# Layer B's queries, keys and P^T turned by VectorE and moved through DRAM, its q/k block number 3 projected sooner, and group 0's scores of layer A in full fp32

## The chip, the cores and the metric

The kernel runs on one core of a Trainium2 chip. The core has a matrix engine (TensorE, PE in the profile, with its weight loads shown as PEld), a vector engine (VectorE, DVE), a scalar engine (ScalarE, ACT), a general engine (GpSimd, POOL) and a queue, SyncE (SP), that issues nearly all DMA transfers here. The engines run side by side, each through its own instructions in order, and wait for each other by semaphores. The metric is the time of one execution on the device in microseconds; the time before is 845.8 us, the median of 3 runs (845.26 to 847.01).

## The reference

A block of two layers on 512 tokens of 1024 features, 16 heads of 64 in fp32. Each layer normalises x, projects it, mixes tokens by attention, multiplies with silu(gate), projects back and adds to x.

```python
def mixer_a(hn, w_in, w_out, q_gain, k_gain, t5_bias):
    proj = hn @ w_in                       # 3 groups of q, k, v and one gate
    for g, (window, dilation) in enumerate(((128, 1), (512, 4), (2048, 16))):
        q = rms_norm(qkv[:, :, g, 0], q_gain[g])
        k = rms_norm(qkv[:, :, g, 1], k_gain[g])
        o, lse = dilated_group_attention(q, k, v, t5_bias[...], dilation, reach)
    y = sum over g of softmax(lse over g) * o
    return (y * silu(gate)) @ w_out

def mixer_b(hn, w_in, w_out, q_gain, k_gain, rpb):
    q, k, v, gate = split(hn @ w_in, 4)    # q and k are normalised per head
    # tokens lie on an 8 x 64 grid; a query sees all 8 rows and a window of 16 columns
    logits = q . k + bias(row offset, column offset)
    p = softmax(logits)
    return ((p @ v) * silu(gate)) @ w_out
```

## The kernel before

The 16 heads are worked in 8 pairs (`hc` 0 to 7), a pair being 128 columns. Layer A is done pair by pair (`main_a`); layer B projects blocks in the order of `B_PARTS` (lines 38 to 41): "qk" i is q and k of pairs 2i and 2i+1 (512 columns), "v" i is v of four pairs, "gate" i is one pair's gate. Each projection contracts 8 steps of 128 rows.

Weights come from DRAM as blocks of 128 x 1024 floats (`wraw`, three buffers, line 184). Each half of a block is split in two parts that TensorE multiplies in its reduced fp32 form (`float32r`): a high part `wh` by ScalarE (line 132) and the rest `wl` by VectorE or GpSimd (line 138), four buffers each. A product is then three matmuls, high x high, high x low and low x high (`mm3`; `mm3_heads` for the two heads of a pair, each on 64 rows of the array). A few products are in full fp32 with unsplit operands.

TensorE's order is written out by hand. Two generators run against each other: `main` issues the projections and output products, `side` issues the attention. A clock kept by the program (`matmul`, `transpose`) adds a planned time per TensorE instruction, and `side` goes on when that clock has reached a due time: `yield "wait", key, delay` waits for a stamp plus a delay in planned nanoseconds. `later_on(delay, job)` puts work of other engines (a transfer, a scaling) at such a time. The order of the other engines is made by a scheduler, apart from instructions pinned with `keep_in_program_order`. A transfer on SP waits in its place in the queue until what it needs is there, and everything behind it waits too.

Layer A, per pair: the projected q is normalised, turned in 32 x 32 blocks by VectorE (`turn_q`), written to DRAM and read back (`move_q`), which leaves it transposed; pairs 6 and 7 are turned by TensorE instead (`transpose4`, line 219). Group 0's q and k are then split (`split_q`, `put_k`) into `q0h`, `q0l`, `k0h`, `k0l`, and scored with `mm3_heads`; groups 1 and 2 are scored in full fp32 with 32 queries a matmul, eight matmuls side by side on 64 x 32 parts of the array. `scores(u)` handles half of the tokens, so that there are 16 such units in the layer. P is turned by VectorE, sent to DRAM and read back into `pt` (`turner`, lines 770 to 783); pair 7's is turned by TensorE. `weigh` multiplies P^T with v (tile `o`).

Layer B, per pair (`side_b`): queries and keys (`raw`) are transposed by TensorE, four transposes each, into PSUM; ScalarE and VectorE read them from there, reordering the grid (`mid_rc`, `edge_rc`) and splitting into high and low parts; two units of scores follow, then softmax. P^T goes through DRAM for pairs 0 to 5 (`far`); for 6 and 7 TensorE transposes P (`turn_p`) and VectorE copies it to `pt` (line 1131). The bias of a pair is read by `bias_b` in six transfers from two small tables (lines 748 and 753). The output product (`out_product`) accumulates k-steps 0 to 6 of seven tiles before step 7, the last pair's, and then the eighth tile in halves.

P's trip in `side_b` reads, with the delays in planned nanoseconds:

```python
                turned.put(pr, 512 if u == 0 else 384, 224 * hd + 128 * u)
            later_on(9000, partial(turned.send, pt[:, :1792], 9500, 1200))
            pending.append(lambda: put_y(hc, weigh(), False, False))
```

Of the kernel before, what the change touches and what calls it, by code (L numbers as in the profile page):

```python
# [27 lines left out]
KT = 8  # L28
# [11 lines left out]
    ("qk", 2), ("v", 1), ("qk", 3), ("gate", 4), ("gate", 5), ("gate", 6), ("gate", 7),  # L40
# [6 lines left out]
def tile_hybrid_encoder(  # L47
# [26 lines left out]

    mid_rc = lambda t: sb(t, 64, [[128, 3], [1, 8], [8, 16]])
    edge_rc = lambda t: sb(t, 0, [[448, 2], [1, 8], [8, 8]])
    mid_q = lambda t: sb(t, 0, [[128, 3], [16, 8], [1, 16]])
    edge_q = lambda t: sb(t, 384, [[64, 2], [8, 8], [1, 8]])
    mid_o = lambda t: sb(t, 64, [[128, 3], [16, 8], [1, 16]])
    edge_o = lambda t: sb(t, 0, [[448, 2], [8, 8], [1, 8]])  # L80
    mid_cr = lambda t: sb(t, 64, [[128, 3], [1, 16], [16, 8]])
    edge_cr = lambda t: sb(t, 0, [[448, 2], [1, 8], [8, 8]])
    mid_n = lambda t: sb(t, 64, [[128, 3], [8, 16], [1, 8]])
    edge_n = lambda t: sb(t, 0, [[448, 2], [8, 8], [1, 8]])

# [12 lines left out]
    lb_d = dr.tile([P, 376], F32, name="lb_d")  # L98
    gb_d = dr.tile([P, 248], F32, name="gb_d")
# [41 lines left out]
    def blocks():  # L141
# [10 lines left out]
        yield from outs(A_OUT)  # L152
# [5 lines left out]
        yield from outs(B_OUT)  # L158

    def outs(b):  # L160

        for n, ks in ((512, KT - 1), (384, KT - 1), (512, 1), (384, 1), (128, KT)):
            yield b, n, ks
            b += n * ks
# [86 lines left out]
    def project(stat_h, stat_l, n, evac, guard, need=None):  # L251

        acc = {i: ps_acc.tile([P, 512], F32, tag="acc", name="acc") for i in range(4)}
        for k in range(KT):
# [5 lines left out]
            h, l = next(wsteps)  # L260
            if need and k == 0:
# [21 lines left out]

    def squares(v, ss, i, ns):
        sq = wk.tile([P, 512], F32, tag="sq", name="sq")[:, : ns * 64]
        if len(v.shape) == 3:
            v = v.rearrange("p (a f) r -> p a f r", f=4)
            nc.gpsimd.tensor_mul(sq.rearrange("p (f a r) -> p a f r", f=4, a=4), v, v)
# [6 lines left out]
    later = []  # L295

    def head_norm(raw, ss, ns, held, delay=0, quick=False):

# [4 lines left out]
        def scale():  # L303
            for i in range(4):
                by = rs[:, i * ns : (i + 1) * ns].unsqueeze(2)
                if len(raw.shape) == 4:
                    v = raw[:, :, i, :].rearrange("p (h a f) r -> p f h a r", h=2, f=4)
                    by = rs[:, i * ns : (i + 1) * ns].rearrange("p (f h) -> p f h", h=2)
                    by = by.unsqueeze(3).unsqueeze(4).to_broadcast([P, 4, 2, 2, 32])
# [4 lines left out]
                if held or delay:  # L314
                    tc.keep_in_program_order(m)

        if held:
            later.append(scale)
        elif delay:
            later_on(delay, scale)  # L320
        else:
            scale()
# [108 lines left out]
    def bias_rows():  # L431

        rp = wk.tile([P, 248], F32, tag="sq", name="rp")
        tc.keep_in_program_order(nc.sync.dma_start(rp, rpb))
        nc.gpsimd.tensor_scalar(rp, rp, -1.0, None, op0=ALU.mult)
        lb = wk.tile([P, 376], F32, tag="sq", name="lb")
        nc.gpsimd.memset(lb, BIG)
        nc.gpsimd.tensor_copy(lb[:, 15 * 8 : 31 * 8], rp[:, 7 * 8 : 23 * 8])
        nc.sync.dma_start(gb_d, rp)
        nc.sync.dma_start(lb_d, lb)  # L440

    st = {}
    pq = wk.tile([P, 4096], F32, tag="pt", name="pt", bufs=1)
    rk = wk.tile([P, 4608], F32, tag="rawk", name="rawk", bufs=1)
# [6 lines left out]
    def project_qk(n, ns, key, hc, guard, first=False, **kw):  # L451

        box = []

        def evac(i, acc):
            if not box:
                if key == "rawq":
# [3 lines left out]
                        if moved(hc)  # L461
# [5 lines left out]
                elif key == "v":  # L467
                    box.append(rk[:, 4 * n * hc : 4 * n * hc + 4 * n].rearrange("p (i c) -> p i c", i=4))
                else:
                    t = wk.tile([P, 4 * n], F32, tag="rawq", name=key, bufs=1)  # L470
                    box.append(t.rearrange("p (i c) -> p i c", i=4))
                box.append(None if key == "v" else wk.tile([P, 32], F32, tag="ss", name="ss"))
            raw, ss = box
            if key == "rawq" and moved(hc):
# [11 lines left out]
            if not first and key != "v":  # L486
                squares(raw[:, :, i, :] if key == "rawq" and moved(hc) else raw[:, i, : ns * 64], ss, i, ns)
# [10 lines left out]
        if key == "raw":  # L498

            ss2 = wk.tile([P, 32], F32, tag="ss", name="ss")  # L500
            for i in range(4):
                squares(raw[:, i, 256:], ss2, i, 4)
            head_norm(raw[:, :, :256], ss, 4, hc % 2 == 1, quick=True)
            head_norm(raw[:, :, 256:], ss2, 4, False, (16500, 16500, 14000, 16000)[hc])
            for n in range(2):
                st[key, 2 * hc + n] = raw[:, :, 256 * n : 256 * n + 256]
# [4 lines left out]
    def normed(raw, ss, ns, key, hc):  # L511
        head_norm(raw, ss, ns, False, 9000 if key == "rawk" and 0 < hc < NHC - 1 else 0)
# [63 lines left out]
    def q_tiles():  # L576
# [3 lines left out]
            wk.tile([P, 512], F32R, tag="q0h", name="q0h", bufs=1),  # L580
            wk.tile([P, 512], F32R, tag="q0l", name="q0l", bufs=1),
            wk.tile([P, 4, 4, P], F32, tag="q12", name="qt", bufs=1),
            wk.tile([P, EXT], F32R, tag="k0h", name="k0h", bufs=1),
            wk.tile([P, EXT], F32R, tag="k0l", name="k0l", bufs=1),
        )

    def q_a(hc):
# [6 lines left out]
        st["q", hc] = q0h, q0l, qt, k0h, k0l = q_tiles()  # L594

        tp = transpose4(raw, 0)
        nc.scalar.copy(tjr(q0h), to_tjr(tp))
        nc.vector.tensor_sub(tjr(q0l), to_tjr(tp), tjr(q0h.bitcast(F32)))
        yield
        tp = transpose4(raw, 3 * P)  # L600
        put_k([(trj(k0h[:, 64:EXT]), trj(k0l[:, 64:EXT]), to_trj(tp))], 0)
# [7 lines left out]
    def move_q(hc, raw):  # L609
# [3 lines left out]
        qt, left = tiles[2], [4]  # L613
# [25 lines left out]
    def split_q(q0h, q0l, qt, k0h, k0l):  # L639
        src = qt[:, :, 3, :].rearrange("p t (j r) -> p t r j", j=4)  # L640
        trj4 = lambda t: t[:, 64:EXT].rearrange("p (t r j) -> p t r j", t=4, j=4)
# [705 lines left out]
```

## Time and profile before

| | |
|---|---|
| time, median of 3 runs | 845.8 us (845.26 to 847.01) |
| span of the profiled execution | 843.7 us |
| what lies around the span, against the median | 2.1 us |
| TensorE busy | 837.7 us, 99% |
| VectorE / ScalarE / GpSimd busy | 528.4 / 427.8 / 294.2 us |
| DMA traffic | 141.20 MB, 167 GB/s mean |
| layer B, first projection to the end | about 569 to 844 us |

The span is the time from the first to the last instruction of one profiled execution; the page gives no other time of that execution. Rows of instruction groups name the line, the engine, the operation, out<-in by the program's names, shapes and a count, then busy time and mean duration, then the idle time of the engine before them and what ended it. In a timeline a row begins with start and duration in microseconds. The chain is the work followed back from the last instruction: at each step to what released it. The waits say which engine's line waited for which other line: total, times, longest.

### The profile page before, as it was taken

What the parts mean: (1) busy time and instruction counts of PE and PEld (TensorE: products, weight loads), DVE (VectorE), ACT (ScalarE), POOL (GpSimd) and SP (SyncE); (2) the same over time, 40 slices, a digit from 0 to 9 for tenths busy, and PEclk for the clock granted to TensorE, in tenths of its full rate; (3) what the DMA queues carried; (4) which work ended last, traced back from release to release, by engine and by line L of the source; (5) the groups of instructions that cost most, each with busy time, mean ns of one, the idle gap of its engine ahead of it and who ended that gap; (6) DMA issues with size and microseconds to landing.
All of it is one profiled execution on the core that took longest, in us unless ns stands there. A gap on an engine that the chain in (4) does not pass through costs nothing.

```text
span 843.7 us, 14965 instructions
## 1 busy us (share of the span) xinstructions
PE 837.7 (99%) x5378; PEld 676.3 (80%) x5378; DVE 528.4 (63%) x1371; ACT 427.8 (51%) x899; POOL 294.2 (35%) x432
## 2 busy tenths in 40 slices
PE   9999999999999999999999999999999999999998
PEld 7788888788788788788788787888878877777777
DVE  7354684684674674675674675447565777668653
ACT  7432653563553653652653564344366465664541
POOL 3352442452441541542532341121521625235211
PEclk9999999999999999999999999999999999999999
DMA  6345478378378278378276364164236546447323
GB/s 253 112 132 178 150 215 248 139 212 259 124 213 258 98 227 246 95 235 244 92 220 189 115 195 110 60 233 176 78 102 197 155 145 191 121 150 202 102 92 131
DMA packets 64218, 141.20 MB, mean 167 GB/s; under 512 B 5648, under 2 KB 23248, under 8 KB 64144
## 3 DMA queue, kind: packets, MB, share of 16 engines
q1 hardware_dynamic: 64000, 139.99, 54.0%
q8 instruction: 42, 0.69, 0.3%
q10 hardware_dynamic: 144, 0.26, 0.1%
q14 instruction: 32, 0.26, 0.1%
HBM read 109.11 MB, written 31.12 MB: 166 GB/s over the span
## 4 chain that ended last, share of the span: by engine, by line
PE 95%; DMA 2%; ACT 1%; DVE 1%; issue 0%; SPq 0%; ACTq 0%
PE acc L215 80%; PE log L215 5%; PE o L215 5%; PE tp L219 3%; DMA pt<-td 1%; DMA wraw<-in_w 1%; DVE hn_l L403 1%; ACT p L1119 1%; DMA x_all<-in_xt 0%; ACT p L694 0%; DVE pt L1017 0%; PE pa L215 0%; ACT raw L485 0%; PE pl L215 0%; PE pk L215 0%
## 5 line engine op out<-in xcount | busy, mean ns | idle before, releaser
L132 ACT CAST wh<-wraw 128x512 fp32r<-128x512 f32 (+1 forms) x259 | 158.3, 612 | 283.5 <-PE acc L215 246.0
L215 PE MATMUL acc<-wh,hn_h 128*128 128x512 f32 x704 | 282.4, 402 | 1.1 <-ACT hn_h L402 0.7
L215 PE MATMUL acc<-wh,hn_l 128*128 128x512 f32 x704 | 274.2, 390 | 0.0
L215 PE MATMUL acc<-wl,hn_h 128*128 128x512 f32 x704 | 274.1, 390 | 0.0
L138 POOL TENSOR_TENSOR wl<-wraw,wh 128x512 fp32r<-128x512 f32 (+1 forms) x104 | 135.2, 1300 | 366.1 <-ACT wh L132 344.5
L138 DVE TENSOR_TENSOR wl<-wraw,wh 128x512 fp32r<-128x512 f32 (+1 forms) x156 | 111.8, 717 | 146.4 <-ACT wh L132 145.3
L215 PEld LDWEIGHTS acc<-wh,hn_h 128*128 128x128 f32 x704 | 132.1, 188 | 35.8 <-issue 5.6
L215 PEld LDWEIGHTS acc<-wh,hn_l 128*128 128x128 f32 x704 | 132.2, 188 | 28.6
L215 PEld LDWEIGHTS acc<-wl,hn_h 128*128 128x128 f32 x704 | 132.4, 188 | 25.2 <-POOL wl L138 0.3
L215 PE MATMUL acc<-y,wh 128*128 128x512 f32 (+1 forms) x272 | 82.5, 387 | 0.0
L215 PE MATMUL acc<-hn_h,wh 128*128 128x512 f32 x192 | 76.1, 396 | 0.0
L215 PE MATMUL acc<-hn_h,wl 128*128 128x512 f32 x192 | 74.9, 390 | 0.0
L215 PE MATMUL acc<-hn_l,wh 128*128 128x512 f32 x192 | 74.8, 389 | 0.0
L694 ACT ACTIVATE p<-p,mn 128x512 f32<-128x512 f32 (+3 forms) x128 | 69.4, 585 | 0.6 <-DVE mn L693 0.2
L857 ACT ACTIVATE p<-p,mn 128x512 f32<-128x512 f32 (+1 forms) x64 | 44.8, 701 | 46.8 <-DVE mn L846 46.5
L291 DVE TENSOR_REDUCE ss<-sq 128x4 f32<-128x256 f32 (+1 forms) x96 | 48.3, 505 | 30.1 <-POOL sq L290 18.7
L770 DVE STREAM_TRANSPOSE tr<-p 128x512 f32<-128x512 f32 (+1 forms) x80 | 53.7, 683 | 12.3 <-ACT p L694 11.6
L215 PEld LDWEIGHTS acc<-y,wh 128*128 128x128 f32 x272 | 48.1, 189 | 9.6 <-issue 1.3
L215 PE MATMUL acc<-y,wl 128*128 128x512 f32 (+1 forms) x136 | 51.4, 378 | 0.0
L215 PEld LDWEIGHTS acc<-hn_h,wh 128*128 128x128 f32 x192 | 36.1, 188 | 8.0 <-issue 0.3
L215 PEld LDWEIGHTS acc<-hn_h,wl 128*128 128x128 f32 x192 | 36.0, 188 | 7.7
L215 PEld LDWEIGHTS acc<-hn_l,wh 128*128 128x128 f32 x192 | 36.1, 188 | 7.0
(143 smaller groups left out, 1041.1 us busy)
## 6 DMA issues: line engine op xcount, KB each, us to landing
wraw<-in_w SPq DMA_DIRECT2D x119, 512.0 KB
td<-tr SPq DMA_DIRECT2D x14, 1024.0 KB
pt<-td SPq DMA_DIRECT2D x56, 256.0 KB
qd<-rawq SPq DMA_DIRECT2D x6, 1024.0 KB
qt<-qd SPq DMA_DIRECT2D x24, 256.0 KB
td<-tr SPq DMA_DIRECT2D x6, 896.0 KB
pt<-td SPq DMA_DIRECT2D x24, 224.0 KB
e<-l_d SPq DMA_DIRECT2D x32, 112.0 KB
```

What stands on the lines that cost most here:

```text
L132: nc.scalar.copy(h, raw)
L138: eng.tensor_sub(l, raw, h.bitcast(F32))
L215: nc.tensor.matmul(o, l, r, **kw)
L219: nc.tensor.transpose(o, i, ident)
L291: nc.vector.tensor_reduce(ss[:, i * ns : (i + 1) * ns], sq.rearrange("p (a b) -> p a b", b=64), axis=AX.X, op=ALU.add)
L403: return nc.vector.scalar_tensor_tensor(l, xk, g, h.bitcast(F32), op0=ALU.mult, op1=ALU.subtract)
L694: nc.scalar.activation(pr, pr, AF.Copy, scale=mn[:, 3:4])
L770: nc.vector.transpose(dst, src[:, :n].rearrange("p (i b k) -> p i b k", b=4, k=32))
L857: nc.scalar.activation(row, row, AF.Exp, bias=mn[:, 1:2], scale=-1.0, accum_out=mn[:, 2:3])
L1119: nc.scalar.activation(pr[:, o : o + n], pr[:, o : o + n], AF.Exp, bias=mn[:, 0:1], scale=-1.0, accum_out=mn[:, 2:3])
```

## The change

1. *Layer B's queries and keys.* The projected block is laid out in 32-column blocks like layer A's q. For each pair VectorE turns it in 32 x 32 blocks in place (two stream transposes of 128 x 512), SP writes it to DRAM (`bd`) and reads it back in four transfers into a tile `landing`, where q and k lie transposed (`move_b`). The second pair of a block follows at a delay. ScalarE and VectorE split from `landing`; the eight q/k transposes of a pair on TensorE are gone. k's low part is made in four pieces, and a copy of q's first 64 tokens is appended, so that tokens stay in one order and the output is multiplied with the gate in one instruction.
2. *Layer B's P^T.* Pairs 6 and 7 go through DRAM as well; their products with v come between the steps of the output product, which now keeps the last two steps back (`late` 2).
3. *Order.* In `B_PARTS`, whose numbers count from 0, "qk" 3 stands behind a gate (24 matmuls) instead of behind "v" 1 (96 matmuls), and "v" 1 follows it. The delays of `side_b` are new.
4. *Projections and output product.* In the first two k-steps the fourth accumulator's matmuls come after the other three's.
5. *Bias of layer B.* During layer A 32 small transfers write a full table to DRAM (`eb_d`); each pair's bias is then read in one transfer instead of six.
6. *Layer A, group 0.* q and k are no longer split; the scores are full-fp32 products in the form of groups 1 and 2, with 256 or 192 columns of keys.

```diff
 B_PARTS = (
     ("qk", 0), ("v", 0), ("gate", 0), ("gate", 1), ("qk", 1), ("gate", 2), ("gate", 3),
-    ("qk", 2), ("v", 1), ("qk", 3), ("gate", 4), ("gate", 5), ("gate", 6), ("gate", 7),
+    ("qk", 2), ("gate", 4), ("qk", 3), ("v", 1), ("gate", 5), ("gate", 6), ("gate", 7),
 )
...
             h, l = next(wsteps)
+            if k < 2 and not need:
+                held.append((h, l))
+                for i in range(3):
+                    mm3(acc[i][:, :n], stat_h(k, i), stat_l(k, i), h, l, k == 0, False)
+                    yield
+                for j, (h, l) in enumerate(held if k else ()):
+                    mm3(acc[3][:, :n], stat_h(j, 3), stat_l(j, 3), h, l, j == 0, False)
+                    yield
+                continue
...
+        for c in range(16):
+            o = 120 - 8 * c
+            g = (56 if c < 8 else 120) - 8 * (c % 8)
+            later_on(15000 + 12000 * c, partial(write, 8 * c, 0, lb[:, o : o + 256]))
+            later_on(21000 + 12000 * c, partial(write, 8 * c, 256, rp[:, g : g + P]))
+    MOVE = 6000, 5500
...
-            head_norm(raw[:, :, :256], ss, 4, hc % 2 == 1, quick=True)
-            head_norm(raw[:, :, 256:], ss2, 4, False, (16500, 16500, 14000, 16000)[hc])
+            move = [partial(move_b, raw, 2 * hc + f) for f in range(2)]
+            head_norm(raw, ss, 4, 0, True, pair=0, then=move[0])
+            head_norm(raw, ss2, 4, (16500, 15000, 10000, 14000)[hc], pair=1, then=move[1])
...
+    def move_b(raw, hc):
+        n = hc % 2
+        blocks = raw.rearrange("p (a f) i r -> p a (f i r)", f=4)[:, :, 256 * n : 256 * n + 256]
+        for a in (0, 2):
+            nc.vector.transpose(blocks[:, a : a + 2], blocks[:, a : a + 2])
+        d = dr.tile([4, P, 256], F32, name="bd", tag="bd", bufs=2)
+        if "landing" not in st:
+            st["landing"] = wk.tile([P, 2, 4, 2, P], F32, tag="q12", name="landing", bufs=1)
+        place, left = st["landing"][:, n], [4]
+        def write():
+            tc.keep_in_program_order(nc.sync.dma_start(d.rearrange("a p x -> p a x"), blocks))
+            stamp["qk", hc] = 0
+        def read(a):
+            dst = place[32 * a : 32 * a + 32].rearrange("k t f x -> k t (f x)")
+            src = d[a].rearrange("(t k) x -> k t x", t=4)
+            tc.keep_in_program_order(nc.sync.dma_start(dst, src))
+            left[0] -= 1
+        later_on(MOVE[0], write)
+        for a in (0, 2, 1, 3):
+            later_on(MOVE[0] + MOVE[1], partial(read, a))
...
-                mm3_heads(
-                    [lg[:, cs : cs + n] for lg in lgs],
-                    lambda hs: q0h[hs, qs], lambda hs: q0l[hs, qs],
-                    lambda hs: k0h[hs, ks], lambda hs: k0l[hs, ks], False,
-                )
+                parts = [(0, j, slice(cs, cs + n), k0, ks) for j in range(4)] + [
+                    (1 + g, j, slice(256 + P * g, 384 + P * g), k12[:, g, :], slice(P * j, P * j + P))
+                    for g in range(2)
+                    for j in range(4)
+                ]
...
-        tp = transpose4(raw, 0)
-        for src, dst in ((mid_rc(tp), mid_q(qh)), (edge_rc(tp), edge_q(qh))):
-            nc.scalar.copy(dst, src)
...
+        nc.scalar.copy(tokens(qh), src(0))
+        nc.scalar.copy(first(qh), landed[:, 0:2, 0, 0:32])
+        nc.vector.tensor_sub(tokens(ql), src(0), tokens(qh.bitcast(F32)))
+        nc.gpsimd.tensor_copy(ql[:, S:EXT], ql.bitcast(F32)[:, 0:64])
+        yield 700
+        scaled(tokens(kh), src(1), 3)
+        for t in range(4):
+            nc.vector.scalar_tensor_tensor(
+                tokens(kl)[:, t], src(1)[:, t], gk[:, 3:4], tokens(kh.bitcast(F32))[:, t],
+                op0=ALU.mult, op1=ALU.subtract,
+            )
+        yield 3800
...
-        for args in held:
-            turn_p(*args)
-            yield 1000
...
+        ready, back, pace = (9000, 9500, 1200) if hc < NHC - 2 else (8000, 5500, 700)
+        later_on(ready, partial(turned.send, pt[:, :1792], back, pace))
+        pending.append(lambda: put_y(hc, weigh(), False, hc == NHC - 1))
...
+            if hc >= 6:
+                yield from weigh_b(hc, (35500, 48500)[hc - 6])
+        stamp["yb", "turned"] = 0
+        for hc, delay in ((NHC - 2, 59000), (NHC - 1, 68500)):
+            yield from weigh_b(hc, delay)
+            yield from residual(xm_d, 4 * (hc % 2))
```

More of the change, by code (lines that the diff above doesn't have):

```diff
@@ L293, in squares, with head_norm @@
         )
-    later = []
-    def head_norm(raw, ss, ns, held, delay=0, quick=False):
+    def head_norm(raw, ss, ns, delay=0, quick=False, pair=None, then=None):
         rs = wk.tile([P, 32], F32, tag="rs", name="rs")
@@ L313, in scale @@
                 m = nc.vector.tensor_mul(v, v, by)
[L314 removed]
+                if delay:
                     tc.keep_in_program_order(m)
[L317 to L319 removed]
+            if then:
+                then()
+        if delay:
             later_on(delay, scale)
@@ L790, in attn_a @@
         e0, e12 = st.pop(("e", hc))
-        q0h, q0l, qt, k0h, k0l = st.pop(("q", hc))
+        qt, k0 = st.pop(("q", hc))
         k12, v12 = st.pop(("k12", hc))
@@ L982, in out_product @@
             acc[f] = ps_acc.tile([P, 512], F32, tag="acc", name="acc")
-        for k in range(KT - 1):
+        held = []
+        for k in range(KT - late):
             chore(True)
             yield key, k, "y"
+            if k < 2:
+                held.append(next(wsteps))
+                yield from step(k, range(3), held[k])
+                for j in range(2 * k):
+                    yield from step(j, (3,), held[j])
+                continue
             yield from step(k, range(4))
```

257 lines of the change are left out of this document (102 added, 155 removed).

## The prediction

> **What bounds the kernel now.** I read the page's busy times and its chain first, then TensorE's groups by shape, then its timeline around the instructions that the change touches, last the chain and the queue SP (the one that issues nearly all transfers) in layer B.
>
> ```profile
> span 843.7 us, 14965 instructions
> PE 837.7 (99%) x5378; PEld 676.3 (80%) x5378; DVE 528.4 (63%) x1371; ACT 427.8 (51%) x899; POOL 294.2 (35%) x432
> PEclk9999999999999999999999999999999999999999
> PE 95%; DMA 2%; ACT 1%; DVE 1%; issue 0%; SPq 0%; ACTq 0%
> ```
>
> TensorE is busy 99% of the span and 95% of the chain that ends last is its own work, at the full granted clock. The span is therefore the sum of TensorE's instructions, and a microsecond of them taken away is a microsecond gained, as long as nothing makes TensorE wait. In layer B it waited for a transfer once:
>
> ```profile
> L219 PE MATMUL tp<-ident,raw 128*128 128x128 f32 x64 | 9.6, 272 | 0.0
> L215 PE MATMUL o<-pt,rawk 128*64 128x128 f32 x64 | 6.6, 285 | 0.8 <-DMA pt<-td 0.8
> L219 PE MATMUL tp<-ident,p 128*128 128x128 f32 x28 | 4.4, 272 | 0.0
> ```
>
> These are TensorE's groups from 570 us on, which is layer B: count, then busy time and mean, then idle time before. All 64 transposes of queries and keys (`raw`) and the 28 of P^T (`p`, head pairs 6 and 7) go away. The means overlap in the pipeline, so I price them by start times:
>
> ```profile
> 781.15 0.39 PE L215 MATMUL acc<-hn_h,wl 128*128 128x512 f32 x1
> 781.38 0.60 PE L219 MATMUL tp<-ident,p 128*128 128x128 f32 x4
> 781.73 0.48 PE L215 MATMUL acc<-hn_h,wh 128*128 128x512 f32 x1
> 782.05 0.40 PE L215 MATMUL acc<-hn_l,wh 128*128 128x512 f32 x1
> ...
> 784.81 0.40 PE L215 MATMUL acc<-hn_h,wl 128*128 128x512 f32 x1
> 785.04 0.49 PE L219 MATMUL tp<-ident,p 128*128 128x128 f32 x3
> 785.29 0.71 PE L215 MATMUL acc<-y,wh 128*128 128x512 f32 x2
> ```
>
> **The change part by part.** *Transposes off TensorE.* A projection matmul starts 0.23 us after the one before it (781.15 to 781.38). Four transposes take 0.35 us, and the matmul behind them is followed only after 0.32 instead of 0.23: 0.44 us a burst. Three take 0.25 and, with the same 0.09 behind them, 0.34. The 64 of `raw` are 16 bursts of four: 16 x 0.44 = 7.0 us. The 28 of `p` are 4 bursts of four and 4 of three: 1.8 + 1.4 = 3.2 us. Together 10.2 us leave TensorE.
>
> *Group 0's scores in full fp32.* Layer A has 16 such units (8 head pairs, two each); one of before, and a full-fp32 group for scale:
>
> ```profile
> 102.83 0.39 PE L215 MATMUL log<-k0h,q0h 64*128 64x256 f32 x2
> 103.06 0.28 PE L215 MATMUL log<-k0l,q0h 64*128 64x256 f32 x2
> 103.17 0.28 PE L215 MATMUL log<-k0h,q0l 64*128 64x256 f32 x2
> 103.29 0.25 PE L215 MATMUL log<-k0h,q0h 64*128 64x192 f32 x2
> ...
> 103.70 1.18 PE L215 MATMUL log<-k,qt 64*32 64x128 f32 x64
> 104.81 0.50 PE L215 MATMUL acc<-wh,hn_h 128*128 128x512 f32 x1
> ```
>
> ```profile
> 41.20 0.89 PE pa L215 x8
> ```
>
> The split products take 103.70 - 102.83 = 0.87 us. In their place come 16 full-fp32 products in the 64x32 shape of the `k,qt` group, half of 256 columns and half of 192; the profile shows such a product as two instructions. From above: 64 instructions of 128 columns take 1.11 us, 17.3 ns each; stretched with the columns, 16 x 34.7 + 16 x 26.0 = 0.97 us, so +0.10 a unit and +1.6 us in all. From below: four full-fp32 products of 128 columns on the whole array (the second row, of the chain) take 0.89 us, 0.22 each; eight side by side at that rate give 0.44 for a tile of 256 columns and 0.33 for one of 192, 0.78 a unit, so -0.09 and -1.5 us in all. The two ends lie evenly about zero and I take 0.0; both stay in the range.
>
> The Trainium skill speaks against this part: "FP8 and Floating Point Precision", section "TensorE Precision Notes", counts four passes through the array for true fp32. An estimate by that page, four passes for three at the old price of a pass, is 0.87 x 4/3 = 1.16 us a unit, +4.6 us in all, and the sum below would be 841.2; the `k,qt` row disagrees with so high a price (0.97 at most), because eight small products run side by side.
>
> *What moves to VectorE.*
>
> ```profile
> 569.00:844.00 275.00, 270.24 (x1497) 215.80 (x1495) 177.70 (x514) 142.30 (x349) 88.16 (x128) 1.00 0.46 142
> ```
>
> ```profile
> L770 DVE STREAM_TRANSPOSE tr<-p 128x512 f32<-128x512 f32 x12 | 8.5, 712 | 0.4
> L719 DVE TENSOR_TENSOR gt<-gt,o 128x384 f32<-128x384 f32 x8 | 7.6, 949 | 7.4 <-PE o L215 7.3
> L770 DVE STREAM_TRANSPOSE tr<-p 128x384 f32<-128x384 f32 x12 | 6.9, 574 | 2.3 <-ACT p L694 2.0
> L719 DVE TENSOR_TENSOR gt<-gt,o 128x128 f32<-128x128 f32 x8 | 3.2, 403 | 0.0
> L1131 DVE COPY pt<-tp 128x512 f32<-128x512 f32 x4 | 2.8, 688 | 0.6 <-PE tp L219 0.6
> L1131 DVE COPY pt<-tp 128x384 f32<-128x384 f32 x4 | 2.2, 557 | 1.1 <-PE tp L219 0.9
> ```
>
> The first row is layer B's window (PE, weight loads, VectorE, ScalarE, GpSimd, clock, DMA share, GB/s): VectorE works 177.7 of 275 us, 65%. It gains two stream transposes a head pair for q and k (16 x 0.71 = 11.4) and eight of P^T (4 x 0.71 + 4 x 0.57 = 5.1); it loses the eight copies (5.0) and, by multiplying the output in one piece of some 0.69 (the copy of the same size), 8 x (0.95 + 0.40 - 0.69) = 5.3. Splitting k's low part into four adds some 8 x 0.4 (a piece at no more than the 0.40 of the 128-column row, against one whole piece of some 0.7 to 0.8). That is about +9 us, 68%. Cost on the path: none, because TensorE's weights are split ahead of it. The cover is four split pieces of 12 matmuls, 4 x 12 x 0.23 = 11 us; without it, each microsecond of VectorE in front of a weight split would be one of TensorE.
>
> *What moves to DMA.* For each of 8 head pairs one write of 512 KB to DRAM and four reads that bring it back; two more P^T round trips; bias tables built in DRAM in layer A by 32 small writes on SP, which shrink each pair's bias from six transfers to one. Every read waits on SP for its write, and what stands behind it waits too, weight loads first.
>
> ```profile
> SPq L184 <- DVE wl L138: 315.6, 85, 12.4
> SPq L184 <- POOL wl L138: 114.3, 42, 6.9
> SPq L783 <- DMA td<-tr: 55.7, 13, 9.7
> SPq L748 <- DVE mn L1109: 32.8, 6, 8.1
> ```
>
> SP mostly waits because a weight buffer (`wraw`) is not free yet, 430 us in sum: loads are issued as early as three buffers allow. A buffer holds 24 matmuls, 5.5 us, so a load has some 16 us, less 5.7 to land (below), before TensorE lacks it. One wait of 9.7 us, the longest for a P^T write, hides in that; two in a row do not. The 32 small writes cost SP about 0.6 us each, as the bias transfers below, spread over some 190 us of A: hidden the same way.
>
> *Where a stall would go.* The tightest place of before is pair 4's P^T:
>
> ```profile
> 727.96 0.91 PE log L215 x12
> ...
> 752.80 0.60 SPq L748
> 753.45 0.58 SPq L753
> 754.09 0.58 SPq L753
> 754.77 5.69 DMA wraw<-in_w
> 760.48 6.09 DMA pt<-td
> 766.82 1.75 PE o L215 x24
> ```
>
> Its scores start at 727.96, its last read leaves SP at 760.48 behind the bias transfers and a weight load, and lands as TensorE reaches the product at 766.82 (the 0.8 us above). In the changed order about as much TensorE work lies between that pair's scores and its product (129 projection matmuls for 135, one more pair of score groups, two transpose bursts less). The last read now stands behind pair 7's q/k reads and the next pair's 896 KB write. At the page's best slice, 259 GB/s, that write is 3.5 us. Against it, five bias transfers, up to 5 x 0.6 = 3 us of SP, are gone from each pair. So the stall moves by -0.8 to +3.5; I take +1.0, nearer the lower end because both have the same place in the queue. For q and k, from the planner's delays: the last read is issued 5 to 6.5 us before ScalarE wants it and another 4.5 lie before the scores; landing takes up to 6.1. Cost 0; if that cover is gone, ScalarE waits first, then the weight casts behind it.
>
> *The sooner q/k block and the later fourth accumulator* move no instruction count on TensorE; the new order gives pairs 6 and 7 time for their trips: behind pair 7's product, the last, 45 output matmuls, 10 us at 0.23, stand before the first that reads its result. Price 0, unless the trip is longer than the delay; then the last output steps wait for it.
>
> Sum: 843.7 - 10.2 + 0.0 + 1.0 = 834.5 us of span. The median of the three runs, 845.8, is 2.1 above the span; with that the time is **836.6 us**.
>
> **The rivals.**
> (1) *Half eaten by late P^T and q/k.* Several pairs land late as pair 4 does. For it speaks that layer B's transfers had no slack once already; against it, layer B's DMA share is 0.46. With three landings late by 2 us each: 836.6 - 1.0 + 6 = 841.6.
> (2) *Slower, through the in-order queue SP.* Ten new round trips (8 of q and k, 2 of P^T) each make SP wait for a write; a wait of before took 55.7 / 13 = 4.3 us. If half of that reaches TensorE through a late weight load, 10 x 2.15 = 21.5, and the time is 845.8 - 10.2 + 21.5 = 857.1. It decides from 1.0 us a trip on. Against it: 13 such waits of before cost TensorE nothing. The skill's "TensorE: Matmul & The Clock Gate", Part 1, adds that an idle array of over about 3.4 us drops to half clock; no row here shows it, the clock being 1.00 throughout.
> (3) *It does nothing.* The transposes filled time in which TensorE would have waited: 845.8. Against it, the two `tp` rows show idle time 0.0 before them and the matmul behind follows at once.
>
> **How the numbers follow.** Forecast case 0.61; rival 1, 0.20; rival 2, 0.13; rival 3, 0.06. Faster or slower begins at 0.2%, 1.7 us, about what a measurement of this kernel can tell from no change. The forecast and rival 1 are faster: 0.81; rival 3 is same: 0.06; rival 2 slower: 0.13. The range goes from 833.0 (fp32 at its lower end, -1.5, the old 0.8 us stall gone, no new one: 845.8 - 10.2 - 1.5 - 0.8 = 833.3) to 844.0, which takes in rival 1 with another late landing.
>
> **What would show it.** Right: no `tp<-ident,raw` group; `tp<-ident,p` 32; the two kinds of group 0 and group 1/2 scores together near 1.98 us a unit; TensorE 98 to 99% busy; `o` waits for `pt<-td` of 1 to 3 us. Wrong: idle time before `log` or `acc` put down to ScalarE, `landing` or `wraw`; SP's waits on `bd` far over 4 us; score units over 2.1 us; or a granted clock below 1 in B.

## The result and the profile after

The changed kernel takes 855.4 us (median of 4 runs, 854.5 to 856.2), the kernel before 846.2 us beside it (845.3 to 847.0): a ratio of 1.0108, 95% interval 1.0096 to 1.0120. The change costs 9 us; 836.6 us was forecast.

The page of the changed kernel's profile (span, busy times, granted clock in 40 slices, chain by engine):

```profile
span 852.8 us, 15498 instructions
PE 831.3 (97%) x5606; PEld 670.5 (79%) x5606; DVE 526.6 (62%) x1379; ACT 426.2 (50%) x893; POOL 286.6 (34%) x440
PEclk9999999999999999999999999999999999999989
PE 80%; DMA 7%; DVE 6%; ACT 4%; issue 1%; SPq 1%; POOL 1%; ACTq 0%; DVEq 0%; POOLq 0%
```

Its waits of TensorE from 569 us on, but for one of 0.6 us (total, times, longest, all in us but the second), and below them those of the kernel before, which are all it had there:

```profile
PE o L203 <- DMA pt<-td: 5.9, 3, 3.8
PE acc L203 <- ACT rawk L493: 3.9, 1, 3.9
PE acc L203 <- DVE gt L1056: 2.9, 2, 2.1
PE acc L203 <- ACT raw L493: 1.4, 1, 1.4
PE log L203 <- ACT kh L686: 1.0, 1, 1.0
PE log L203 <- DVE k0b L1087: 0.8, 1, 0.8
```

```profile
PE o L215 <- DMA pt<-td: 0.8, 1, 0.8
PE acc L215 <- ACT raw L485: 0.3, 1, 0.3
PE acc L215 <- DVE pt L1017: 0.2, 1, 0.2
```

TensorE's idle time in the span has gone from 843.7 - 837.7 = 6.0 us to 852.8 - 831.3 = 21.5, and 80% of the last chain is its own work where it was 95%. Its busy time hides one thing more: in four windows of 3.4 us (one from 713.9, one from 768.5, two from 823.1) it ran at half the clock. It was busy for 12.7 us of them, so about 6.4 us of the 831.3 are due to the slow clock. At full clock its work is some 824.9 us, 12.8 less than before. So 843.7 - 12.8 + 15.5 + 6.4 = 852.8: the work that was to go has gone, and 22 us of waiting and slow clock came in its place.

TensorE's first `pk` matmul starts at 32.9 us in the traces of before and of the changed kernel and up to 2.2 us later in some others, which shifts everything behind it, so that executions of one kernel differ by some 2 us.

The three largest stalls, each with its cause on the engine it waits for. In the timeline a row has start and duration in us, engine, line, operation, out<-in, and in brackets the idle time before it and what ended it. First, at 710 us, the timeline of TensorE and then of VectorE:

```profile
710.35 0.39 PE L203 MATMUL acc<-wh,hn_l 128*128 128x512 f32 x1
712.79 0.50 PE L203 MATMUL acc<-wh,hn_h 128*128 128x512 f32 x1 [2.05 <-DVE gt L1056]
...
708.60 0.71 DVE L778 STREAM_TRANSPOSE tr<-p 128x512 f32<-128x512 f32 x1
709.42 0.67 DVE L125 TENSOR_TENSOR wl<-wraw,wh 128x512 fp32r<-128x512 f32 x1
710.64 0.57 DVE L778 STREAM_TRANSPOSE tr<-p 128x384 f32<-128x384 f32 x1
711.45 0.58 DVE L778 STREAM_TRANSPOSE tr<-p 128x384 f32<-128x384 f32 x1
712.04 0.69 DVE L1056 TENSOR_TENSOR gt<-acc,rs_half 128x512 f32<-128x512 f32 x1
```

q/k block 3 needs four accumulators. It starts with three and wants the fourth after 18 matmuls, but gate 4 still lies there: the multiply that empties it (line 1056) runs at 712.04, behind the softmax, the stream transposes and the head norms that stand ahead of it in VectorE's order. Second, at 763 us, the timeline of TensorE and then of ScalarE:

```profile
763.17 0.39 PE L203 MATMUL acc<-wh,hn_l 128*128 128x512 f32 x1
767.43 0.50 PE L203 MATMUL acc<-hn_h,wh 128*128 128x512 f32 x1 [3.87 <-ACT rawk L493]
...
763.40 0.50 ACT L1133 ACTIVATE p<-p,mn 128x256 f32<-128x256 f32 x1
763.90 1.89 ACT L713 ACTIVATE p<-p,mn 128x256 f32<-128x256 f32 x4
765.70 0.60 ACT L119 CAST wh<-wraw 128x512 fp32r<-128x512 f32 x1
766.20 0.51 ACT L1133 ACTIVATE p<-p,mn 128x256 f32<-128x256 f32 x1
766.71 0.67 ACT L493 ACTIVATE rawk<-acc,rs_n 128x512 f32<-128x512 f32 x1
```

v block 1 is ready and holds all four accumulators, but its copies out of PSUM (line 493) stand behind pair 5's softmax (lines 1133 and 713) on ScalarE. Third, the last product at 820 us, the timeline of the queue SP and then of TensorE:

```profile
811.93 0.32 SPq L1026 DMA_DIRECT2D pt<-xm_d  x1
812.30 0.42 SPq L791 DMA_DIRECT2D pt<-td  x1
812.77 0.42 SPq L1026 DMA_DIRECT2D pt<-xm_d  x1
813.24 0.91 SPq L791 DMA_DIRECT2D pt<-td  x2
815.48 0.43 SPq L791 DMA_DIRECT2D pt<-td  x1
...
819.88 0.39 PE L203 MATMUL acc<-y,wl 128*128 128x512 f32 x1
824.07 3.26 PE L203 MATMUL o<-pt,rawk 128*64 128x128 f32 x24 [3.80 <-DMA pt<-td]
```

Two 512 KB reads of the residual (line 1026) stand among pair 7's four P^T reads (line 791); the first of them had to wait for pair 6's product. The last P^T read landed at 823.8, 8.3 us after it was issued behind the queue's other transfers, and TensorE stood still for it.

### The profile page after: what moved, and what is told of

Same layout as the page of the kernel before. It is cut to its first block, busy times and chain, and to the rows that moved or that the text cites. A ratio compares the mean times of both kernels' runs of the same rounds, so it can differ in the third digit from the quotient of the medians.

```text
span 852.8 us, 15498 instructions
## 1 busy us (share of the span) xinstructions
PE 831.3 (97%) x5606; PEld 670.5 (79%) x5606; DVE 526.6 (62%) x1379; ACT 426.2 (50%) x893; POOL 286.6 (34%) x440
## 4 chain that ended last, share of the span: by engine, by line
PE 80%; DMA 7%; DVE 6%; ACT 4%; issue 1%; SPq 1%; POOL 1%; ACTq 0%; DVEq 0%; POOLq 0%
PE acc L203 68%; PE o L203 5%; PE log L203 4%; DMA pt<-td 3%; PE tp L207 2%; DMA bd<-raw 2%; DMA landing<-bd 2%; SPq L661 1%; DVE raw L312 1%; ACT wh L119 1%; ACT raw L493 1%; DVE wl L125 1%; ACT p L1133 1%; DVE raw L648 1%; DVE ssq L1043 1%
## 5 line engine op out<-in xcount | busy, mean ns | idle before, releaser
L125 DVE TENSOR_TENSOR wl<-wraw,wh 128x512 fp32r<-128x512 f32 (+1 forms) x156 | 117.4, 753 | 163.3 <-ACT wh L119 163.2
L778 DVE STREAM_TRANSPOSE tr<-p 128x512 f32<-128x512 f32 (+1 forms) x88 | 58.6, 679 | 10.9 <-ACT p L713 9.6
```

The costliest lines, as they stand in the source:

```text
L125: eng.tensor_sub(l, raw, h.bitcast(F32))
L778: nc.vector.transpose(dst, src[:, :n].rearrange("p (i b k) -> p i b k", b=4, k=32))
```

## The experiments

The theories. 1: the trips through DRAM cost the time themselves. 2: VectorE's turning of q and k does. 3: the order does: evacuations of accumulators stand in the in-order queues of VectorE and ScalarE behind softmax work that the new delays put right ahead of them, and at the end P^T reads stand behind the residual's on SP. 4, a form of 2: VectorE and ScalarE have too much to do there whatever its order.

**Layer A's part alone** (`a_alone`). The kernel before, with group 0's scores in full fp32 and nothing else.

> The kernel before with one part of the change alone: group 0's scores of layer A in full fp32. TensorE of the changed kernel has 837.7 - 831.3 = 6.4 us less busy time and its clock was granted at 0.992 of 852.8 us, so at full clock its work is some 13 us less, of which the transposes explain 10.2. Theory: this part gains the other 3 us; time 3 us below the kernel before, some 843. Rival: it costs nothing and gains nothing, as I had priced it (0.0, from -1.5 to +1.6); then the time is that of the kernel before within 1.6 us.

Measured: 843.2 us (843.0 to 845.2), ratio 0.9962 (0.9950 to 0.9975). One scoring unit in the timeline of the changed kernel, and the instruction behind it:

```profile
102.75 1.99 PE L203 MATMUL log<-k,qt 64*32 64x256 f32 x96
104.66 0.50 PE L203 MATMUL acc<-wh,hn_h 128*128 128x512 f32 x1
```

This unit takes 104.66 - 102.75 = 1.91 us where it took 1.98; of the 16 units six take about as long and ten 1.84, 29.9 us in sum where they took 31.8. The last one comes 2.0 us sooner after the first `pk` (531.95 - 35.05 = 496.9 in this kernel's trace, 531.76 - 32.85 = 498.9 before). The medians, 843.2 and 847.1 beside it, are 3.9 us apart, but hold different starts: between the lowest runs lie 2.4 us (843.0 and 845.4), between the highest 2.5 (845.2 and 847.7). Layer A's part is a gain of 2.0 to 2.5 us, so layer B's parts cost some 12 us against it.

**Theories 1 and 2** (`no_trip`, `no_turn`). The changed kernel without the five transfers of each q/k trip, and without VectorE's 16 stream transposes of q and k (both leave the scores meaningless).

```diff
-            tc.keep_in_program_order(nc.sync.dma_start(d.rearrange("a p x -> p a x"), blocks))   # no_trip, and the reads
-            nc.vector.transpose(blocks[:, a : a + 2], blocks[:, a : a + 2])                      # no_turn
```

> The changed kernel without the transfers of layer B's queries and keys: VectorE still turns them, but they are neither written to DRAM nor read back; the split parts are made from a tile filled once with a constant, so layer B's scores are not those of the reference. Theory 1, the trips through DRAM (the waits for landing on ScalarE and VectorE, and the queue that P^T shares with them) make most of TensorE's 15.5 us of new idle time: the idle time falls from 21.5 us to under 12, and the time to 845 or less. Theory 2, VectorE's added work makes it: the time stays above 851.

> The changed kernel without VectorE's 16 stream transposes of layer B's queries and keys (10.3 us of VectorE): the trips through DRAM stay, what lands isn't transposed, so layer B's scores are not those of the reference. Theory 1 (the trips): the time stays within 2.5 us of the changed kernel, 853 to 857. Theory 2 (VectorE's added work): most of the idle time goes and the time is 848 or less.

Measured: 854.9 us (850.8 to 855.3) and 856.8 us (856.0 to 858.7). Neither gives the time back. Without the transfers the small stalls at the landings go, but three large ones stay, even in the profiled execution, which was the fastest of the four (850.8 us):

```profile
PE acc L203 <- DVE gt L1052: 5.3, 2, 4.7
PE acc L203 <- ACT rawk L493: 3.9, 1, 3.9
PE o L203 <- DMA pt<-td: 3.4, 1, 3.4
```

Without the stream transposes one stall is exchanged for another: `gt` has only 0.9 us of waits, but the evacuation of q/k block 2 (`raw`, line 493) now takes 4.4, and `rawk` (3.9) and the last `pt<-td` (3.8) stay. As single causes both theories fall, theory 1 as far as the trips of q and k go; those of P^T follow below.

**The residual's place on SP** (`resid_late`). The changed kernel, residual reads behind pair 7's product and pinned there in SP's order.

```diff
         for hc, delay in ((NHC - 2, 59000), (NHC - 1, 68500)):
             yield from weigh_b(hc, delay)
-            yield from residual(xm_d, 4 * (hc % 2))
+        for half in range(2):
+            yield from residual(xm_d, 4 * half)
```

> The changed kernel with one order on the queue SP undone: the first half of the residual is read for the output only after pair 7's P^T has been read, as pinned transfers, instead of ahead of it. In the changed kernel these two reads of 512 KB wait on SP for pair 6's product (until 811.9 us) and pair 7's four reads of P^T stand behind them and land at 823.8, 4.2 us after TensorE wants them. Theory: the last stall of 4.2 us goes and with it the half clock behind it (about 1.7 us): 849 to 850. Rival: the amount of transfer alone sets the landing and the order doesn't matter: 853.5 or more.

Measured: 850.4 us (849.1 to 852.0), 5.0 less than the changed kernel, just above the 849 to 850 expected. Its last product starts without a wait, in this row of its timeline:

```profile
822.24 1.75 PE L203 MATMUL o<-pt,rawk 128*64 128x128 f32 x24
```

Its last P^T read landed 4.4 us after its issue instead of 8.3. It was issued at the same point of the kernel (817.5, with a start 2.1 us later, against 815.5), so SP's waiting had not held it up. That stall is shown: it is the order on one queue, and the megabyte that went ahead.

**The two evacuations** (`gate4_free`, `v1_free`), each on top of `resid_late`: scores planned later, so that they stand behind the evacuation.

```diff
-        yield "wait", ("raw", hc), (18000, 33000, 18000, 30000, 20500, 33000, 23000, 34000)[hc]
+        yield "wait", ("raw", hc), (18000, 33000, 18000, 38000, 20500, 33000, 23000, 34000)[hc]   # gate4_free
+        yield "wait", ("raw", hc), (18000, 33000, 18000, 30000, 20500, 46500, 23000, 34000)[hc]   # v1_free, and later products of pairs 4 and 5
```

> Edit to the version with the late residual reads (850.4 us): pair 3's scores are planned 8 us later (raw delay 38000 for 30000), so that they stand behind gate block 4 on TensorE and gate 4's multiply stands ahead of pair 3's softmax on VectorE. Nothing else changes. Theory 3 (order on the in-order VectorE and ScalarE queues): the 2.4 us stall of acc on gt at 712 goes, and with it some 1.7 us of half clock behind it if that window is due to it; 850.4 - 2.2 - 1.7 = 846.5 us (845.5 to 848). If VectorE simply has too much to do in B (throughput), the same work is still there and the stall moves: 849.5 to 851.

> Edit to the version with the late residual reads (850.4 us): pair 5's scores are planned 13.5 us later (raw delay 46500 for 33000; pair 5's product 54500 for 48500 after its stamp), so that v1's four evacuations stand ahead of pair 5's softmax on ScalarE. Theory 3: the 4.9 us stall of acc on rawk at 765 goes and the 6.8 us window of half clock behind it too: 850.4 - 4.7 - 3.4 = 842.3 us (841 to 845; pairs 5 to 7 then have some 2.5 us less for their P^T, which may give back 1 to 2). If the stall is VectorE's and ScalarE's throughput or their q/k work, it moves: 849 to 852.

Measured: 854.9 us (854.2 to 856.2) and 853.2 us (852.5 to 854.9); both misses, and slower than `resid_late`. Of the waits of TensorE from 570 us on the longest and the one for `gt`, `gate4_free`:

```profile
PE o L203 <- DVE tr L778: 10.4, 1, 10.4
PE acc L203 <- DVE gt L1058: 0.8, 1, 0.8
```

and the two largest in `v1_free`:

```profile
PE o L203 <- DMA pt<-td: 6.9, 3, 3.0
PE acc L203 <- DVE gt L1058: 6.3, 3, 3.8
```

In each the stall aimed at is gone (no wait of over 0.8 us for `gt` in the first, none for `rawk` in the second). In `gate4_free` pair 3's product, left in its place, waited 10.4 us for a P^T that now started 8 us later. In `v1_free` the stall for `gt` at 711 stays as in `resid_late`, and two come that it did not have: another gate's multiply ended a wait of 3.8 us at 790, and pair 7's P^T one of 3.0 at 825. From these I estimated that a pair needs some 36 us of planned time from its scores to its product. In the traces the trip is longer: a product that waited began 47.5 us after its pair's scores in the changed kernel (pair 2, 682.4 to 729.9), and 44.6 in `gate4_free` (pair 3, 709.5 to 754.1).

**The old order, and q/k alone in it** (`order_back`, `qk_only`).

```diff
-    ("qk", 2), ("gate", 4), ("qk", 3), ("v", 1), ("gate", 5), ("gate", 6), ("gate", 7),   # both
+    ("qk", 2), ("v", 1), ("qk", 3), ("gate", 4), ("gate", 5), ("gate", 6), ("gate", 7),
-        turned = turner(448)              # qk_only, pairs 6 and 7: back to turn_p
```

> The changed kernel with only the order of B's blocks put back (v block 1 ahead of q/k block 3, gate 4 behind it) and the delays that go with it; q/k and all P^T still go through VectorE and DRAM, A's group 0 in full fp32. Theory 3: no evacuation of a v or gate block stands behind the softmax of the pair scored just before, so the stalls at 710 and 763 (2.4 + 4.3 us, and some 5 us of half clock) are gone; what comes new is that pairs 6 and 7 have 15 us less for their trips at the end: 840 to 847 us. If the trips or VectorE's work are the cause whatever the order: 852 or more.

> The order of before, P^T of pairs 6 and 7 transposed by TensorE as before, A's group 0 in full fp32; queries and keys of B turned by VectorE and moved through DRAM as in the changed kernel. Against A's part alone (843.2 us) this takes 16 bursts x 0.44 = 7.0 us off TensorE. Theory 3: the trips themselves cost little in the old order, a few landing waits of 1 us each: 837 to 841 us. If the q/k trips or the work they bring VectorE and ScalarE are the cause: 846 or more.

Measured: 865.0 and 870.4 us, both far off, and no verdict on the order: in both I had planned pair 2's product 31 us after its scores, and it waited 13.2 us for its P^T, with half clock behind it; it began 47.5 us after its scores in both, as in the changed kernel. What they show is the price of too short a trip. Neither waited over 0.9 us for `gt` or `rawk`, which is what theory 3 said of the old order, but a stall of 13 us also gives the other engines time to catch up.

**Scores and products spaced** (`score_first`, `spread`, `spread2`), on top of `resid_late`: pairs 4 and 5 are scored ahead of the products of pairs 2 and 3; in the other two pair 3 is scored 8 us later; in `spread` pair 2 is 2 us later; in `spread2` pair 3's product is 7.5 us later.

```diff
-        yield "wait", ("raw", hc), (18000, 33000, 18000, 30000, 20500, 33000, 23000, 34000)[hc]
+        yield "wait", ("raw", hc), (18000, 33000, 18000, 38000, 20500, 31000, 23000, 34000)[hc]   # spread2
...
-            if hc >= 6:
-                yield from weigh_b(hc, (35500, 48500)[hc - 6])
+            if hc >= 4:
+                yield from weigh_b(hc, (29000, 50000, 35500, 48500)[hc - 4])
```

> Edit to the version with the late residual reads (850.4 us): pairs 4 and 5 are scored ahead of the products of pairs 2 and 3 and not behind them (pair 5 from 31000 for 33000 after its stamp; products of pairs 2 and 3 planned at 29000 and 42500). Every pair then has at least 36 us from its scores to its product, and pair 5's softmax is over before v1's evacuations come. Theory 3, with the amendment from the last four runs that a P^T trip needs some 36 us and a shorter one stalls its product: the 4.9 us stall at 765 and the 6.8 us of half clock behind it go, and the 2.7 us stall of pair 2's product at 729 too: 850.4 - 4.7 - 3.4 - 2.5 = 839.8 us (839 to 843). Rival theory 4 (VectorE and ScalarE have too much work around 750 to 770 us, whatever its order): the stall comes back elsewhere, 847 to 852.

> As score_first, and pair 3 is scored 8 us later (38000 for 30000), behind gate block 4, its product having been moved by as much already; pair 2 is scored 2 us later (20000 for 18000), when its queries and keys have landed. Theory 3: the 2.4 us stall at 712 goes too, and the 2.0 us of waiting for pair 2's landing at 683 and the half clock there (1.7): 839.8 - 2.2 - 2.0 - 1.7 = 834 us, say 834 to 839. Rival theory 4: 847 or more.

> As score_first (848.1 us), with pair 3 scored 8 us later, behind gate block 4 (38000 for 30000), and its product 7.5 us later still (50000 for 42500), so that its P^T has its 36 us; pair 2 stays at 18000. Theory 3: the 2.4 us stall at 713 and the 1.7 us of half clock behind it go, no new one comes: 848.1 - 2.2 - 1.7 = 844.2 us (843 to 846). Theory 4 (too much work for VectorE and ScalarE around the q/k splits): 848 or more.

Measured: 848.1 us (846.6 to 849.7), 848.3 us (847.1 to 849.7) and 842.4 us (841.4 to 844.1; ratio 0.9959, 0.9945 to 0.9972). `score_first` missed its 839 to 843: the stall for `rawk` only shrank, from 4.5 us in `resid_late` to 2.5, and the one for `gt` stayed. `spread2` came out below its 843 to 846. It does all of the changed kernel's work with other delays and one queue order, 13 us faster, so theory 4 falls as an explanation of those 13 us. `spread` missed: it lost 5.7 us at pair 3's product, which then got its time in `spread2`, and 4.1 at the evacuation of q/k block 2. What is left in `spread2`, the three largest waits from 569 us on:

```profile
PE acc L203 <- ACT rawk L493: 3.6, 2, 3.3
PE log L203 <- ACT kh L686: 1.3, 1, 1.3
PE log L203 <- DVE k0b L1089: 0.8, 1, 0.8
```

**The waits that are left** (`spread3`, `spread5`, `spread4`). In `spread2`, ScalarE's cast of pair 6's q waited for its landing until 763.4, and v1's copies behind it. `spread3` pins that pair's casts behind the copies and scores it 3.5 us later; `spread5` 4 us later still (and pair 7 2 us later); `spread4` is `spread5` with pair 2 scored 1 us later.

```diff
+                    if key == "v" and hc == 1:
+                        tc.keep_in_program_order(m)
...
+        if hc == 6:
+            tc.keep_in_program_order(m)
```

> As spread2 (842.4 us), with pair 6's casts of q and k kept behind v1's four evacuations on ScalarE, and its scores planned 3.5 us later (26500 for 23000; products of pairs 6 and 7 then 2.5 and 3 us later, 61500 and 71500). Theory 3: the 3.3 us stall of acc on rawk at 762 goes: 842.4 - 3.3 = 839.1 us (838 to 840.5). If VectorE's work there is the cause: 842 or more.

> As spread3 (846.1 us), with pair 6's scores planned 4 us later still (30500 for 26500), so that its casts of q and k, which stand behind v1's evacuations, are done before TensorE comes to them; the products of pairs 6 and 7 move by as much. Theory 3: neither the stall of acc on rawk at 762 nor that of log on kh at 769 is there: from spread2's 842.4 us, 842.4 - 3.3 = 839.1 us (838 to 841). If VectorE's and ScalarE's work always brings one back: 842 or more.

> As spread5, with pair 2 scored 1 us later (19000 for 18000), between the two values tried. Theory 3: its waits for the landing at 683 fall by 1 us, which takes the idle time in one window of the clock under some 2 us and with it the half clock behind it (1.7 to 3.4): 835 to 838 us. If the wait only moves to the evacuation of q/k block 2 behind pair 2's softmax, as in spread: 839 or more.

Measured: 846.1 us (844.1 to 847.6), 842.3 us (841.0 to 845.6) and 844.1 us (841.9 to 845.5); three misses. In `spread3` the wait for `rawk` is gone and two others, the largest there, stand in its place:

```profile
PE log L203 <- ACT kh L688: 4.3, 2, 2.5
PE log L203 <- DVE k0b L1097: 2.1, 2, 1.3
```

The casts now came too late for the scores. In `spread4` pair 2's wait for its landing fell, and the evacuation of q/k block 2 waited 3.4 us behind its softmax, as in `spread`. No version tried has a median below 842: every wait that was taken away came back at a neighbour, and whether a better plan exists is left open.

**P^T of pairs 6 and 7 alone** (`p_only2`), on top of `a_alone`; a first form, `p_only`, with later products and residual reads, computed a wrong output, and its 851.3 us answer nothing.

```diff
-    far = lambda hc: hc < NHC - 2
+    far = lambda hc: True
...
+        for hc, delay in ((NHC - 2, 50000), (NHC - 1, 57500)):
+            yield from weigh_b(hc, delay)
         yield from residual(xm_d)
```

> A's group 0 in full fp32 (843.2 us alone) and P^T of pairs 6 and 7 turned by VectorE and moved through DRAM, the last two rows of B's output weights kept to the end; queries and keys of B transposed by TensorE, the order of B's blocks and the other delays as before; the residual is read behind pair 7's product, as early as its buffer allows. It takes the 28 transposes of p, 3.2 us, off TensorE. Theory 3 (a P^T trip with enough time to its product costs nothing): 840.0 us (839 to 842). If such trips cost TensorE time as such: 845 or more.

Measured: 843.4 us (841.5 to 843.8), a miss (839 to 842 was expected), with a median no different from that of layer A's part alone. Its waits from 570 us on are these three:

```profile
PE acc L217 <- DVE gt L1040: 0.6, 1, 0.6
PE acc L217 <- ACT raw L487: 0.3, 1, 0.3
PE acc L217 <- DVE pt L1015: 0.2, 1, 0.2
```

The trips of P^T cost TensorE no wait, and its last matmul starts 2.5 us sooner than in `a_alone` (837.4 against 839.9; 0.2 of it is the start). But the span ends 4.5 us after that matmul starts, not 3.5, since the residual's reads now come late: 1.5 us of span are left. The runs agree, though the medians, with different starts in them, do not show it: the lowest and the highest are 1.5 and 1.4 us below those of `a_alone`.

The fastest of all are `spread5` (842.3), `spread2` (842.4), `a_alone` (843.2) and `p_only2` (843.4); by their medians they cannot be told apart, and each is about 0.4% faster than the kernel before and 1.4 to 1.5% faster than the changed one. The later fourth accumulator and the bias tables were not run alone; from 30 to 570 us TensorE is busy for 540.0 us in both kernels, so the tables' writes cost it no wait there. Whether the old block order, with delays that leave P^T its time, would do as well is open too.

## Why the prediction was wrong

The forecast span was 834.5 us, the measured one 852.8. Of the 18.3 us between them, 7.7 are waits for accumulators to be emptied, 6.4 the slow clock, 4.1 waits for P^T beyond the 1.8 us that the forecast held, 1.8 waits for the landing of q and k, and 0.9 small waits. Those are 20.9; against them, 2.6 us more work left TensorE than was forecast.

*Transposes off TensorE, 10.2 us: right.* Of the 12.8 us that TensorE's work lost, layer A's part has 2.0 by the traces; 10.8 are left for the transposes.

*Group 0 in full fp32, 0.0 between -1.5 and +1.6: mis-sized.* It gave 2.0 us in the traces and up to 2.5 between like runs, more than the lower end: even the price from below, 0.78 us a unit, was too high. The estimate by the Trainium skill's "FP8 and Floating Point Precision", "TensorE Precision Notes" (four passes, +4.6 us), is contradicted by the units of 1.84 and 1.92 us.

*VectorE's 9 us cost nothing: not refuted as an amount, but wrong in its reason.* Without 10.3 us of its work (`no_turn`) the time is no shorter, and with all of it and other delays it is 13 us shorter (`spread2`). VectorE's busy time in the prediction's window grew by less than forecast, from 177.7 to 183.6 us:

```profile
569.00:853.00 284.00, 264.06 (x1396) 209.51 (x1394) 183.60 (x536) 141.25 (x346) 88.92 (x135) 0.98 0.60 177
```

The reason given was that weights are split ahead of TensorE. They are: TensorE waited nowhere for `wl` or `wraw`. What stood in the same queues with no such cover was the emptying of the accumulators, gate 4's multiply on VectorE and v1's copies on ScalarE: 2.1 and 3.9 us, with 1.7 of half clock behind each. I had asked what is queued behind the added work and had looked at weights alone.

*The sooner q/k block and its order, price 0: wrong, and this is the main step that failed.* The prediction looked at TensorE's instruction count and at the time for the last trips, and not at what the order puts ahead of the evacuations. Its place and the new delays put the softmax of pairs 3 and 5 right ahead of them. Other delays and one queue order, with the same work and the same block order, gave 13 us back (855.4 to 842.4), 5.0 of them by the residual's reads alone. The text's one condition, a trip longer than its delay so that the last output steps wait, did come true at 820 us, for 3.8 us and 2.9 of half clock; its cause, the residual's reads on SP among pair 7's, was not in the working.

*P^T, +1.0 between -0.8 and +3.5: mis-sized.* The three waits for `pt<-td` are 5.9 us. Pair 4's, the one priced, was within its range (1.2 us at 783, 0.8 before); pair 2's, 1.0, and pair 7's, 3.8, were not in the sum.

*The q/k trips, cost 0: too low.* The waits for `kh` and `k0b` behind pair 2's landing are 1.8 us. In `spread2` they are 2.1 with 6.8 us of half clock behind them, which cost 3.2 more: half of the 10.4 us of waiting and slow clock that are left there. "If that cover is gone, ScalarE waits first, then the weight casts behind it" named the right engine and the wrong victim.

*Rival 2*, slower through SP, came near in time (857.1), but by luck, since its mechanism did little: no late weight load, but one late P^T read, 5 us of the 22.

*The clock.* "No row here shows it" held for the trace of before; the changed kernel's rows show it, and a 2.1 us stall was enough (below). The prediction put no price on a stall beyond its length. A clock below 1 in B (0.98 in the row above) was one of its own signs of being wrong, and so was idle time before `acc` and `log` put down to ScalarE (3.9, 1.4 and 1.0 us); both came.

## What to carry to other kernels

When work moves from the bound engine to an in-order helper, list everything in that helper's queue that the bound engine waits for, evacuations of accumulators as well as operands, and look at where each will stand and not only at the helper's busy share. A trip through DRAM needs its time again at every later step: a pair whose scores moved and whose product did not, or whose delay was too short, waited 10 to 13 us, as much as the transposes were worth or more. A gain that comes with new waits is best judged stage by stage, since here one part of the change (layer A's) gave as much as the whole of it with the best delays tried.

## What the runs showed of the hardware

TensorE's clock falls to half for whole windows of 3.41 us that lie on a fixed grid in each execution (in the changed kernel they begin at 713.9, 768.5 and 823.1 us, 54.6 apart, which is 16 windows), and whether a stall costs that depends on where it lies on the grid. The changed kernel's stall at 710 us and nearly the same stall in `v1_free`, by windows (TensorE's busy time is the second figure after the comma, the clock the figure after GpSimd's):

```profile
710.50:713.90 3.40, 1.35 (x7) 0.94 (x6) 3.35 (x13) 1.54 (x4) 1.94 (x8) 1.00 0.63 212
713.90:717.30 3.40, 3.40 (x10) 2.63 (x9) 3.01 (x5) 1.13 (x2) 3.02 (x7) 0.50 0.26 89
```

```profile
711.10:714.50 3.40, 1.70 (x7) 1.42 (x8) 3.32 (x10) 1.59 (x5) 2.39 (x10) 1.00 0.51 159
714.50:717.90 3.40, 3.40 (x16) 2.82 (x15) 2.99 (x6) 1.24 (x2) 2.60 (x6) 1.00 0.44 145
```

Both stalls are 2.4 us between starts. In the first, 2.05 us of it lie in one window and the next runs at half clock, 10 matmuls in it where the one before the stall had 17. In the second the window's edge divides it, 1.70 us are idle, and the clock stays. Over all 18 traces, of the full-clock windows from 60 us on with TensorE idle for 1.9 us or more, all 25 were followed by one at half clock; of 22 with 1.5 to 1.9 us, 5; of 40 with 0.7 to 1.5, none. So a stall of 2 to 4 us costs itself and often 1.7 us more. The Trainium skill's "TensorE: Matmul & The Clock Gate", Part 1, gives a free-running window of 3413 ns, and the grid agrees; that it takes a whole idle window does not: 1.9 us idle, 56% of one, was always enough, and 1.6 sometimes.

A write of 512 KB to DRAM on the trip of q and k took 2.9 to 7.0 us to land and the four reads behind it 2.3 to 5.4 each (`spread2`), while the last P^T read of 224 KB took 4.4 us in `resid_late` and 8.3 in the changed kernel, behind a megabyte of other reads.
